# A four-layer encoder and a sparse-attention block on one core: later probability transposes, other banks for the attention results, a searched order of issue

## The chip, the cores and the metric

The kernel runs on one core of a Trainium2 chip as one launch. The metric is the device time of one execution in microseconds. Every time of the kernel before in this document comes from its measured runs or from the profile and the trace of one profiled execution.

## What is computed

The input is one sequence of 256 tokens of width 1024. Four layers follow each other; each is a mixer and a gated feed-forward net of hidden width 2816, with a layer norm behind either. The mixers are attention within a band of chunks (layers 0 and 3, 16 heads of 64), a gated linear attention with a running state (layer 1), and differential attention (layer 2, 8 pairs of maps, whose second map is taken off with a learned weight). Cut from the reference:

```
for i in range(DEPTH):
    if kind == 0:   y = chunk_band_attention(h, a_w_qkv[j], a_rel_bias[j], a_w_o[j])
    elif kind == 1: y = gated_linear_attention(h, ...)
    else:           y = differential_attention(h, ...)
    h = layer_norm(DN_ALPHA * h + y, ln1_g[i], ln1_b[i])
    h = layer_norm(DN_ALPHA * h + swiglu(h, ...), ln2_g[i], ln2_b[i])
```

A second block takes the result: a feed-forward net, then a mixer that picks for every query the 64 best keys by an index score and attends to these alone, beside a short convolution; then cross attention to 256 memory rows, and a last feed-forward net. All weights are float32 and are read once, in some 600 transfers of 512 KB.

## The kernel before

The 256 tokens are two tiles of 128, `tt` 0 and 1. `stream(tt)` (L1019) is a generator that writes down all the work of one tile, layer by layer, and gives control back after every quarter of a weight unit. `run` (L1053) lets tile 0 go ahead of tile 1: the lead grows from `LAG0` = 1 step by one step for every `LAGK` = 4 steps of tile 1, up to `LAG` = 6 (L32, L33).

A weight quarter is 512 KB. One SP transfer brings it into one of 5 `raw` buffers (L268); ACT copies it to `wh` in the fast fp32r format (L276), DVE takes the rest `wl` = raw - wh (L277), each in one of 10 buffers. The activations are split alike (`sth`, `stl`; `gth`, `gtl`). A product is then three matmuls of 128 x 512 (`mm3`, L288, L290, L292). `lin` (L294) makes 512 columns of a projection, `lin_out` (L310) the 1024 columns of an output projection. PSUM has eight banks: four with the tag `acc` for `lin_out`, two `lin` for `lin`, and two `at` for transposes and scores (L250). With a tag, banks are opened in the order in which the program was written down.

Attention for a group of heads goes like this in `mixer_attn` (L658). After the projection "q", the queries are transposed (`to_heads`). Then, twice (sub 0 and 1), `attn_probs` (L603) makes the scores of four heads in two `at` banks (L613, a burst that nothing may break up), adds the bias and takes the maximum on DVE (L619), takes the exponential on ACT (L624), and scales on DVE (L629, or L685 and L687 in layer 2); and at once `transpose_probs` (L632, matmul L641) turns the probabilities `p` over into `pt`. After the projection "v", the result `o` is made in a `lin` bank (L707, L715) and copied out of it (`bank_to_gt`, L350; in layer 2 to `t`, L720, with a norm behind it: squares L723, L530, a power on POOL L363, L534, L727). The gated layer keeps its result in a `lin` bank too (L804), and so does the cross attention (L1006). `mixer2` (L842) has the selecting attention: eight rounds of maximum and replace on DVE (L911, L912), then scores and probabilities as above, transposed at once and used after the projections "bo" and "sb0".

The order in which instructions are issued isn't the written one. `order_issue` (L1393) reads all instructions, and `plan_order` (L1162) makes a graph of them. `play` (L1227) plays the program once with fixed durations: the engine that can start first takes, of up to 24 candidates, the one with the earliest deadline. Deadlines are counted back from the times at which PE has to do its matmuls. `play` is run four times, the PE order of one round setting the deadlines of the next, and the best round's order is fixed for every engine. A transfer counts as its bytes by 360 per ns, whatever its rows (L1087). All transfers share SP's queue; loads that are not weights are the bias tiles (`b<-toep`, L483, 128 KB each, rows of 256), the bias tables in DRAM (`toep<-t`, L469), the norms' gains and offsets (`bc`, L369, 512 KB) and some small constants.

Of the kernel before, what the change touches and what calls it, by code (L numbers as in the profile page):

```python
# [32 lines left out]
LAG0, LAGK = 1, 4  # L33
# [176 lines left out]
class Net:  # L210
# [83 lines left out]
    def lin(self, st, key):  # L294
# [4 lines left out]
        for a in range(u.nq):  # L299
# [10 lines left out]
    def lin_out(self, gt, key, accs, first, last):  # L310
# [3 lines left out]
        for a in range(u.nq):  # L314
# [6 lines left out]
            if a == u.nq - 1:  # L321
                for b, wh, wl in kept:
                    self.mm3_out(gt, b, accs, (1,), wh, wl, first and b == 0, last and b == u.nq - 1)
            yield
# [333 lines left out]
    def mixer_attn(self, tt, st, i):  # L658
# [3 lines left out]
        for g in range(2):  # L662
# [8 lines left out]
            probs = []  # L671
            for sub in range(2):
# [7 lines left out]
                if diff:  # L680
# [17 lines left out]
            o = self.bank("lin")  # L698
# [36 lines left out]
    def mixer_gla(self, tt, st, i):  # L735
# [42 lines left out]
        for pr in range(2):  # L778
# [19 lines left out]
            o = self.bank("lin")  # L798
# [43 lines left out]
    def mixer2(self, tt, st):  # L842
# [87 lines left out]
        probs = []  # L930
# [52 lines left out]
    def cross(self, tt, st):  # L983
        nc = self.nc
        gts = []
        for g in range(2):
# [16 lines left out]
            o = self.bank("lin")  # L1003
# [84 lines left out]
DMA_BACKLOG = 2500.0  # L1088
TAIL = 10000.0
# [5 lines left out]
class Op:  # L1095
    __slots__ = ("inst", "eng", "dur", "fset", "preds", "succs", "opens", "idx", "dl", "npred", "ready", "start", "end",
                 "burst")
# [56 lines left out]
def _bytes(inst):  # L1154
    o = inst.outs[0]
    n = 4
    for s, c in list(o.ap):
        n *= c
    return n

# [66 lines left out]
def play(ops, users, tag_of, bufs_of, nominal):  # L1227
# [17 lines left out]
    loads = [op.idx for op in ops if op.eng == "SP" and op.inst.outs[0].bass_ap.tensor.name.startswith(("raw", "h0", "h1"))]  # L1245
    for i, j in zip(loads, loads[1:]):
        before[i].append(j)
    for op in reversed(ops):
# [4 lines left out]
        if op.eng == "SP":  # L1253
            d -= DMA_LAND + _bytes(op.inst) / DMA_RATE
# [8 lines left out]
        op.ready = 0.0  # L1263
    slots = {}
    for name, tag in tag_of.items():
        slots.setdefault(tag, [0.0] * bufs_of[tag])
    left = {name: len(u) for name, u in users.items()}
    done_at = {name: 0.0 for name in users}
    touched = [[] for _ in range(n)]
# [23 lines left out]
    def eff(op):  # L1293
# [9 lines left out]
        if op.opens:  # L1303
# [3 lines left out]
            for tag, k in need.items():  # L1307
# [3 lines left out]
                t = max(t, sorted(s)[k - 1])  # L1311
        return t
    while ndone < n:
# [47 lines left out]
        free[e] = t + dur  # L1361
        if e == "SP":
            dma_free = max(dma_free, t + DMA_ISSUE + 650) + _bytes(op.inst) / DMA_RATE
# [4 lines left out]
        order[e].append(i)  # L1368
# [99 lines left out]
```

## Time and profile before

| | us |
|---|---|
| median of 3 runs | 1912.93 |
| lowest to highest | 1912.18 to 1914.75 |
| the profiled execution, its own time | 1910.72 |
| its span, first to last instruction | 1908.9 |
| PE busy | 1873.2 |
| DVE busy | 1177.6 |
| ACT busy | 940.6 |
| mean granted share of PE's clock | 0.995 |

The page gives each engine's busy time. The timeline gives instructions in order of time; in brackets stands how long the engine sat idle before one, and what ended that. The view of stretches gives busy times and the granted clock of PE (1.00 is 2.4 GHz, 0.50 is 1.2 GHz) for pieces of the span. Matmuls are pipelined, so a matmul's own duration is longer than the time from one to the next.

### The profile page before, as it was taken

The page shows a single profiled execution, that of the slowest core. Times are in us where ns is not written, and L with a number is a line of the kernel's source. Part 1 is how long each engine was busy: PE and PEld are TensorE (multiplying, and loading weights), DVE is VectorE, ACT ScalarE, POOL GpSimd, SP SyncE. Part 2 cuts the span into 40 slices and gives each one's busy share as a digit, 9 for nine tenths or more (in the row PEclk, how much of TensorE's full clock was granted, in tenths as well). Part 3 has the DMA queues.
Part 4 walks back from the last instruction along what each step waited for, and adds up shares of the span by engine and source line. Part 5 has one row for each costly group of instructions (what it writes and reads, how often), then busy time and mean ns, then how long its engine had stood idle before and what let it go on. Part 6 is the DMA issues. An engine that isn't in the chain of part 4 may idle for free. (4 is left out here: it accounts for less than half of the span.)

```text
span 1908.9 us, 23804 instructions
## 1 busy us (share of the span) xinstructions
PE 1873.2 (98%) x8941; PEld 1519.8 (80%) x8941; DVE 1177.6 (62%) x1697; ACT 940.6 (49%) x1359; POOL 41.8 (2%) x65
## 2 busy tenths in 40 slices
PE   8899999999999999999999999999999899999998
PEld 7678887678888877888878888888877688788887
DVE  6576556567556777555767655765567867566554
ACT  6545445454444664444564444444445555545442
POOL 0000000000000000000000000000000000000000
PEclk9999999999999999999999999999999999999999
DMA  9546555656554645655554655465554466546662
GB/s 308 157 145 217 188 190 153 207 163 218 186 185 161 209 155 165 196 190 187 185 171 163 209 185 191 160 225 187 188 172 144 134 202 208 163 125 204 184 193 67
DMA packets 103437, 345.59 MB, mean 181 GB/s; under 512 B 13385, under 2 KB 20489, under 8 KB 103322
## 3 DMA queue, kind: packets, MB, share of 16 engines
q1 hardware_dynamic: 103322, 344.07, 56.4%
q8 instruction: 70, 1.15, 0.3%
q14 instruction: 45, 0.37, 0.1%
HBM read 341.01 MB, written 3.01 MB: 180 GB/s over the span
## 5 line engine op out<-in xcount | busy, mean ns | idle before, releaser
L277 DVE TENSOR_TENSOR wl<-raw,wh 128x1024 fp32r<-128x1024 f32 (+2 forms) x614 | 741.3, 1215 | 461.5 <-ACT wh L276 460.4
L276 ACT ACTIVATE wh<-raw 128x1024 fp32r<-128x1024 f32 (+2 forms) x614 | 643.6, 1053 | 640.2 <-PE lin L292 399.6
L288 PE MATMUL lin<-wh,sth 128*128 128x512 f32 x1696 | 665.0, 397 | 4.8 <-DVE t L856 1.3
L290 PE MATMUL lin<-wl,sth 128*128 128x512 f32 x1696 | 656.1, 392 | 1.1 <-DVE wl L277 1.1
L292 PE MATMUL lin<-wh,stl 128*128 128x512 f32 x1696 | 656.8, 393 | 0.0
L288 PEld LDWEIGHTS lin<-wh,sth 128*128 128x128 f32 x1696 | 318.4, 188 | 75.6 <-issue 5.2
L292 PEld LDWEIGHTS lin<-wh,stl 128*128 128x128 f32 x1696 | 318.4, 188 | 70.3 <-issue 5.3
L290 PEld LDWEIGHTS lin<-wl,sth 128*128 128x128 f32 x1696 | 318.8, 188 | 64.5 <-DVE wl L277 2.4
L290 PE MATMUL acc<-wl,gth 128*128 128x512 f32 x752 | 247.7, 394 | 0.0
L288 PE MATMUL acc<-wh,gth 128*128 128x512 f32 x752 | 244.7, 395 | 0.7 <-ACT gth L341 0.7
L292 PE MATMUL acc<-wh,gtl 128*128 128x512 f32 x752 | 245.0, 393 | 0.0
L290 PEld LDWEIGHTS acc<-wl,gth 128*128 128x128 f32 x752 | 141.2, 188 | 30.3 <-DVE wl L277 0.9
L292 PEld LDWEIGHTS acc<-wh,gtl 128*128 128x128 f32 x752 | 140.6, 188 | 30.0 <-issue 1.3
L288 PEld LDWEIGHTS acc<-wh,gth 128*128 128x128 f32 x752 | 140.0, 188 | 30.4 <-issue 1.5
L336 PE MATMUL at<-ident,t 128*128 128x128 f32 x564 | 92.9, 276 | 9.6 <-DVE t L727 2.9
L336 PEld LDWEIGHTS at<-ident,t 128*128 128x128 f32 x564 | 70.1, 142 | 31.7 <-issue 9.3
L593 DVE TENSOR_TENSOR t<-t,lin 128x512 f32<-128x512 f32 x60 | 41.2, 687 | 68.5 <-PE lin L292 68.5
L363 POOL TENSOR_TENSOR sm<-sm,small 128x1 f32<-128x1 f32 (+2 forms) x42 | 37.0, 880 | 1649.9 <-DVE sm L512 917.0
L341 ACT ACTIVATE gth<-at 128x512 fp32r<-128x512 f32 (+1 forms) x88 | 49.5, 563 | 46.8 <-PE at L336 46.7
L624 ACT ACTIVATE p<-p,sm 128x128 f32<-128x128 f32 (+1 forms) x112 | 49.6, 444 | 34.7 <-DVE sm L622 34.7
L342 DVE TENSOR_TENSOR gtl<-at,gth 128x512 fp32r<-128x512 f32 (+1 forms) x88 | 57.2, 650 | 9.9 <-ACT gth L341 6.8
L590 ACT ACTIVATE t<-lin 128x512 f32<-128x512 f32 x60 | 35.8, 596 | 48.7 <-PE lin L292 48.6
(165 smaller groups left out, 859.9 us busy)
## 6 DMA issues: line engine op xcount, KB each, us to landing
raw<-in_weights_dram SPq DMA_DIRECT2D x607, 512.0 KB, 3.6
b<-toep SPq DMA_DIRECT2D x40, 128.0 KB, 5.1
bc<-in_ln_g_dram SPq DMA_DIRECT2D x8, 512.0 KB, 3.8
bc<-in_ln_b_dram SPq DMA_DIRECT2D x8, 512.0 KB, 5.9
toep<-t SPq DMA_DIRECT2D x2, 768.0 KB, 11.6
h<-in_x_dram SPq DMA_DIRECT2D x4, 256.0 KB, 5.8
bc<-in_ffn_post_g_dram SPq DMA_DIRECT2D x2, 512.0 KB, 3.6
p<-in_mem_dram SPq DMA_DIRECT2D x2, 512.0 KB, 6.6
```

Of the source, the lines that this page charges most:

```text
L276: nc.scalar.activation(hi[:, c], src[:, c], AF.Copy)
L277: nc.vector.tensor_sub(lo[:, c], src[:, c], hi[:, c].bitcast(F32))
L288: nc.tensor.matmul(o, xh, w, start=first, stop=False)
L290: nc.tensor.matmul(o, xh, w, start=False, stop=False)
L292: nc.tensor.matmul(o, xl, w, start=False, stop=last)
L336: self.nc.tensor.transpose(b[:, k], src[:, k * 128:(k + 1) * 128], self.ident)
L341: self.nc.scalar.activation(hi, b[:, :n], AF.Copy)
L342: self.nc.vector.tensor_sub(lo, b[:, :n], hi.bitcast(F32))
L363: nc.gpsimd.tensor_tensor(out, x, self.mhalf[:, :x.shape[1]], op=OP.pow)
L590: nc.scalar.activation(gate[j], acc, AF.Silu)
L593: nc.vector.tensor_mul(s, s, acc)
L624: nc.scalar.activation(P[:, hh, :nk], P[:, hh, :nk], AF.Exp, bias=nm[:, hh:hh + 1], accum_out=sm[:, hh:hh + 1])
```

## The change

- The transposes of the probabilities are written later. `mixer_attn` makes both halves' probabilities first and hands a function `turn` to the projection "v", which calls it after its second quarter; in `mixer2` it is called after the last quarter of "bo".
- The results `o` of `mixer_attn`, of the gated layer and of `cross` are in an `at` bank instead of a `lin` bank. In `mixer2` it stays in `lin`.
- `LAGK` is 1, so tile 0's lead grows by a step for each step of tile 1.
- In `play`, a transfer with rows under 512 elements on either side counts at 110 per ns. A load that is neither a weight nor the input isn't issued before 30 us ahead of its deadline.
- `play` is run 60 times. After three rounds, `search` sorts what PE waited for by pieces of 40 us, and in later rounds takes off a random part of these waits from the deadlines of the instructions that caused them; by piece, the best set of such hurries is kept, and the order with the shortest end is used.

The matmuls themselves, the transfers and the work on DVE, ACT and POOL stay the same in number and size. The diff, without bookkeeping (who set an instruction's start, what buffer came free by whom):

```diff
-LAG0, LAGK = 1, 4
+LAG0, LAGK = 1, 1
...
-    def lin(self, st, key):
+    def lin(self, st, key, later=None, after=0):
...
+            if later is not None and a == after:
+                later()
             yield
...
-            probs = []
+            Ps, probs = [], []
...
-                    PT = self.transpose_probs(tt, P, (0, 2))
-                else:
-                    PT = self.transpose_probs(tt, P, range(4))
-                probs.append(PT)
-            acc = yield from self.lin(st, (i, "v", g))
+                Ps.append(P)
+
+            def turn():
+                for P in Ps:
+                    probs.append(self.transpose_probs(tt, P, (0, 2) if diff else range(4)))
+
+            acc = yield from self.lin(st, (i, "v", g), turn, 1)
             v = self.t("v2", [128, 512], 4)
             self.copy(v, acc)
             self.v[g, tt] = v
-            o = self.bank("lin")
+            o = self.bank("at")
...
-            o = self.bank("lin")
+            o = self.bank("at")
...
-            probs.append(self.transpose_probs(tt, P, range(4)))
+            Ps.append(P)
+
+        def turn():
+            for P in Ps:
+                probs.append(self.transpose_probs(tt, P, range(4)))
+
         for which in "ba":
             accs = [self.bank("acc"), self.bank("acc")]
-            yield from self.lin_out(gtb if which == "b" else gta, which + "o", accs, True, True)
+            yield from self.lin_out(gtb if which == "b" else gta, which + "o", accs, True, True,
+                                     turn if which == "b" else None, 3)
...
-            o = self.bank("lin")
+            o = self.bank("at")
...
+SHORT_ROW, SHORT_RATE = 512, 110.0
+HOLD = 30000.0
...
+def _transfer(inst):
+    short = min(list(o.ap)[-1][1] for o in (inst.outs[0], inst.ins[0])) < SHORT_ROW
+    return _bytes(inst) / (SHORT_RATE if short else DMA_RATE)
...
-            d -= DMA_LAND + _bytes(op.inst) / DMA_RATE
+            d -= DMA_LAND + _transfer(op.inst)
+        d -= urge.get(op.idx, 0.0)
...
+        if op.eng == "SP" and op.idx not in first_loads and not raws(op):
+            op.ready = max(0.0, op.dl - HOLD)
...
+def waits_by_region(ops, order):
+
+    behind, res = {}, {}
+    for seq in order.values():
+        for a, b in zip(seq, seq[1:]):
+            behind[b] = a
+    for a, b in zip(order["PE"], order["PE"][1:]):
+        gap = ops[b].start - ops[a].start - ops[a].dur
+        if gap < 20.0:
+            continue
+        r = res.setdefault(ops[b].region, [0.0, []])
+        r[0] += gap
+        i, n = ops[b].blame, 0
+        while gap > 100.0 and i is not None and ops[i].eng != "PE" and n < 40:
+            n += 1
+            if ops[i].blame is None:
+                r[1].append((i, gap))
+                i = behind.get(i)
+            else:
+                i = ops[i].blame
+    return res
+
+
+def search(ops, users, tag_of, bufs_of, nominal, rounds):
+
+    rng = random.Random(1)
+    urge, best = {}, None
+    kept = {}
+    for r in range(rounds):
+        got = play(ops, users, tag_of, bufs_of, nominal, urge)
+        if got is None:
+            break
+        if r < 3:
+            t2 = 0.0
+            for i in got[1]["PE"]:
+                t2 += ops[i].dur
+                nominal[i] = t2
+        if r == 2:
+            for op in ops:
+                op.region = int(op.dl // REGION)
+            for i in got[1]["PE"]:
+                ops[i].region = int(nominal[i] // REGION)
+        if best is None or got[0] < best[0]:
+            best = got
+        if r < 3:
+            continue
+        now = waits_by_region(ops, got[1])
+        tried = {}
+        for i, x in urge.items():
+            tried.setdefault(ops[i].region, {})[i] = x
+        for g in set(now) | set(kept):
+            w, causes = now.get(g, [0.0, []])
+            if g not in kept or w < kept[g][0] - 1.0:
+                kept[g] = (w, tried.get(g, {}), causes)
+        urge = {}
+        for g, (w, us, causes) in kept.items():
+            urge.update(us)
+            if r % 8 and r < rounds - 2:
+                size = rng.choice((0.3, 0.6, 1.0, 2.0))
+                for i, gap in causes:
+                    if rng.random() < 0.5:
+                        urge[i] = urge.get(i, 0.0) + min(gap, 2000.0) * size
+                for i in us:
+                    if rng.random() < 0.1:
+                        urge[i] *= 0.5
+    return best
...
-def order_issue(tc, nc, tag_of, bufs_of, bursts, rounds=4):
+def order_issue(tc, nc, tag_of, bufs_of, bursts, rounds=60):
...
-    best = None
-    for r in range(rounds):
-        got = play(ops, users, tag_of, bufs_of, nominal)
-        if got is None:
-            break
-        if best is None or got[0] < best[0]:
-            best = got
-        t2 = 0.0
-        for i in got[1]["PE"]:
-            t2 += ops[i].dur
-            nominal[i] = t2
+    best = search(ops, users, tag_of, bufs_of, nominal, rounds)
```

The order on PE, in the selecting attention of tile 0, from the second half's scores (L613, L618 in the change) to the transposes of its probabilities (L641, L646). Before:

```order
L613 MATMUL at_12307<-k_2572_11854,q_2673_12270 128x128
L613 MATMUL at_12308<-k_2572_11854,q_2673_12270 128x128
L290 MATMUL acc_12338<-wl_12360,gth_2631_12115 128x512
L292 MATMUL acc_12337<-wh_12359,gtl_2632_12116 128x512
L292 MATMUL acc_12338<-wh_12359,gtl_2632_12116 128x512
L288 MATMUL acc_12337<-wh_12390,gth_2631_12115 128x512
L288 MATMUL acc_12338<-wh_12390,gth_2631_12115 128x512
L641 MATMUL at_12331<-ident_63,p_2686_12313 128x128 x2
L336 MATMUL at_12371<-ident_63,t_2701_12369 128x128 x2
```

With the change, from the first half's scores on; the last row transposes the first half, and the second half follows 8 rows later:

```order
L618 MATMUL at_12277<-k_2572_11854,q_2673_12270 128x128
L618 MATMUL at_12278<-k_2572_11854,q_2673_12270 128x128
L289 MATMUL lin_12367<-wh_12140,sth_2539_11687 128x512
L291 MATMUL lin_12367<-wl_12141,sth_2539_11687 128x512
L293 MATMUL lin_12367<-wh_12140,stl_2540_11688 128x512
L289 MATMUL lin_12367<-wh_12229,sth_2539_11687 128x512
L291 MATMUL lin_12367<-wl_12230,sth_2539_11687 128x512
L618 MATMUL at_12300<-k_2572_11854,q_2673_12270 128x128
L618 MATMUL at_12301<-k_2572_11854,q_2673_12270 128x128
...
L291 MATMUL acc_12324<-wl_12377,gth_2631_12115 128x512
L293 MATMUL acc_12324<-wh_12376,gtl_2632_12116 128x512
L646 MATMUL at_12405<-ident_63,p_2677_12283 128x128 x4
```

The two halves' scores now stand five matmuls apart and ahead of everything that uses them; before, one half was transposed ahead of the next half's scores.

The order on SP in layer 1, the gated layer, where the bias tiles of layer 2 (`b_1115`, `b_1231`), a bias table and the norm's gains (`bc`) were loaded between weights. Before:

```order
L268 DMA raw_2879<-in_weights_dram 128x1024
L483 DMA b_1115_5200<-toep_2592 32x4x256 x3
L268 DMA raw_2897<-in_weights_dram 128x1024
L268 DMA raw_2927<-in_weights_dram 128x1024
L469 DMA toep_2597<-t_561_2594 512x1x384
L483 DMA b_1115_5200<-toep_2592 32x4x256
L268 DMA raw_2945<-in_weights_dram 128x1024
L483 DMA b_1231_5667<-toep_2592 32x4x256 x4
L369 DMA bc_3545<-in_ln_g_dram 128x1024
L369 DMA bc_3547<-in_ln_b_dram 128x1024
L268 DMA raw_2965<-in_weights_dram 128x1024
```

With the change, the same stretch of weights:

```order
L269 DMA raw_2840<-in_weights_dram 128x1024
L269 DMA raw_2879<-in_weights_dram 128x1024
L474 DMA toep_2597<-t_561_2594 512x1x384
L269 DMA raw_2897<-in_weights_dram 128x1024
L269 DMA raw_2927<-in_weights_dram 128x1024
L269 DMA raw_2945<-in_weights_dram 128x1024
L269 DMA raw_2965<-in_weights_dram 128x1024
L269 DMA raw_2983<-in_weights_dram 128x1024
L269 DMA raw_3031<-in_weights_dram 128x1024
```

Bias tiles and gains have left this stretch, and one bias table is left in it.

The order on DVE at the end of layer 2's attention, tile 1: the norm of the second group's result (L530, L534, L727; L535, L539, L734 in the change) and the layer norm of tile 0 (L508 to L512; L513 to L517). Before:

```order
L277 TENSOR_TENSOR wl_6176<-raw_6173,wh_6175 128x1024
L277 TENSOR_TENSOR wl_6194<-raw_6191,wh_6193 128x1024
L530 TENSOR_SCALAR sm_6054<-sm_6048 128x4
L534 TENSOR_SCALAR sm_6058<-sm_6055 128x4
L509 BN_STATS sm_6121<-h_15_77 128x6 x2
L510 BN_AGGR sm_6122<-sm_6121 128x2
L512 TENSOR_SCALAR sm_6129<-sm_6122 128x1
L727 SCALAR_TENSOR_TENSOR t_1325_6046<-t_1325_6046,sm_6058,cst_5000 128x128 x4
```

With the change:

```order
L278 TENSOR_TENSOR wl_6102<-raw_6099,wh_6101 128x1024
L278 TENSOR_TENSOR wl_6158<-raw_6155,wh_6157 128x1024
L535 TENSOR_SCALAR sm_6054<-sm_6048 128x4
L513 SCALAR_TENSOR_TENSOR h_15_77<-h_15_77,acc_5853 128x512
L539 TENSOR_SCALAR sm_6058<-sm_6055 128x4
L734 SCALAR_TENSOR_TENSOR t_1325_6046<-t_1325_6046,sm_6058,cst_5000 128x128 x4
L514 BN_STATS sm_6121<-h_15_77 128x6
L513 SCALAR_TENSOR_TENSOR h_15_77<-h_15_77,acc_5854 128x512
```

The statistics of the layer norm (BN_STATS, BN_AGGR) stood ahead of the scaling of `t`; now they stand behind it.

## Rows read from the trace of the kernel before

**Rows 1.** The page: the span, and PE's busy time with its share.

```profile
span 1908.9 us, 23804 instructions
...
PE 1873.2 (98%) x8941; PEld 1519.8 (80%) x8941; DVE 1177.6 (62%) x1697; ACT 940.6 (49%) x1359; POOL 41.8 (2%) x65
```

**Rows 2.** Stretches: us, each engine's busy us (instructions), PEclk, DMA share, GB/s.

```profile
60.00:70.00 10.00, 6.18 (x38) 5.06 (x38) 3.79 (x13) 3.87 (x11) 0.38 (x2) 0.72 0.60 158
70.00:80.00 10.00, 10.00 (x55) 8.19 (x52) 1.92 (x2) 2.37 (x4) 0.00 (x0) 0.94 0.18 54
340.00:350.00 10.00, 7.52 (x39) 5.75 (x37) 5.04 (x5) 6.97 (x10) 0.31 (x1) 1.00 1.03 361
...
550.00:600.00 50.00, 50.00 (x230) 41.32 (x229) 26.35 (x26) 22.80 (x25) 0.00 (x0) 1.00 0.56 183
...
730.00:740.00 10.00, 7.22 (x28) 5.32 (x29) 8.99 (x18) 3.22 (x5) 0.56 (x1) 0.83 0.11 34
1490.00:1500.00 10.00, 8.77 (x42) 5.94 (x40) 9.56 (x33) 3.19 (x10) 0.00 (x0) 1.00 0.53 156
1500.00:1510.00 10.00, 6.08 (x27) 4.13 (x29) 6.35 (x16) 5.97 (x14) 0.00 (x0) 0.66 0.13 31
```

**Rows 3.** Timeline, PE: start, us, form, count [idle before it <-releaser].

```profile
52.43 0.47 PE L288 MATMUL lin<-wh,sth 128*128 128x512 f32 x1 [1.32 <-DVE gtl L353]
...
56.36 1.23 PE L641 MATMUL at<-ident,p 128*128 128x128 f32 x8 [0.48 <-DVE p L629]
...
64.98 1.30 PE L641 MATMUL at<-ident,p 128*128 128x128 f32 x5 [3.82 <-DVE p L629]
...
349.51 0.65 PE L336 MATMUL at<-ident,t 128*128 128x128 f32 x4 [2.48 <-ACT sm L763]
...
680.08 0.50 PE L288 MATMUL lin<-wh,sth 128*128 128x512 f32 x1 [0.51 <-ACT t L720]
...
732.10 1.02 PE L336 MATMUL at<-ident,t 128*128 128x128 f32 x4 [2.85 <-DVE t L727]
733.81 1.22 PE L288 MATMUL acc<-wh,gth 128*128 128x512 f32 x2 [0.69 <-ACT gth L341]
...
1503.92 0.66 PE L641 MATMUL at<-ident,p 128*128 128x128 f32 x2 [5.15 <-DVE p L629]
```

**Rows 4.** Timeline, all engines: the first of the long stops, 58 to 65 us.

```profile
58.90 1.13 PE L613 MATMUL at<-k,q 64*128 64x256 f32 x8
...
60.07 0.42 DVE L619 CUSTOM_DVE_ANT_0 p<-at,b 128x256 f32<-128x256 f32 x1 [0.38 <-PE at L613]
...
61.83 0.51 ACT L624 ACTIVATE p<-p,sm 128x256 f32<-128x256 f32 x1
...
64.15 1.29 DVE L629 TENSOR_TENSOR p<-p,sm 128x512 f32<-128x512 f32 x2
```

**Rows 5.** Timeline, SP and ACT, 328 to 350 us, layer 1.

```profile
328.90 7.21 SPq L483 DMA_DIRECT2D b<-toep  x4
...
338.02 20.99 SPq L268 DMA_DIRECT2D raw<-in_weights_dram  x9
...
346.92 1.06 ACT L276 ACTIVATE wh<-raw 128x1024 fp32r<-128x1024 f32 x1 [2.85 <-DMA raw<-in_weights_dram]
347.99 1.28 ACT L763 ACT_TABLE_LOAD   x1
```

**Rows 6.** Timeline, ACT, POOL and DVE, 726 to 733 us, the end of layer 2's attention.

```profile
726.62 0.58 ACT L720 ACTIVATE t<-lin 128x512 f32<-128x512 f32 x1
...
728.86 1.01 POOL L363 TENSOR_TENSOR sm<-sm,small 128x4 f32<-128x4 f32 x1 [2.81 <-DVE sm L530]
...
729.98 1.28 DVE L509 BATCH_NORM_STATS2 sm<-h 128x6 f32<-128x512 f32 x2
...
731.61 1.13 DVE L727 SCALAR_TENSOR_TENSOR t<-t,sm,cst 128x128 f32<-128x128 f32 x4
```

**Rows 7.** The page's groups: the weight split on DVE.

```profile
L277 DVE TENSOR_TENSOR wl<-raw,wh 128x1024 fp32r<-128x1024 f32 (+2 forms) x614 | 741.3, 1215 | 461.5 <-ACT wh L276 460.4
```

More of the change, by code (lines that the diff above doesn't have):

```diff
@@ L2 @@
 import math
+import random
 from contextlib import ExitStack
@@ L306, in lin, with lin_out @@
                 self.mm3([acc[:, :n]], st[0][:, kt], st[1][:, kt], [wh[:, s]], [wl[:, s]], kt == 0, kt == 7)
+            if later is not None and a == after:
+                later()
             yield
         return acc
-    def lin_out(self, gt, key, accs, first, last):
+    def lin_out(self, gt, key, accs, first, last, later=None, after=0):
         u = self.by_key[key]
@@ L323, in lin_out @@
                     self.mm3_out(gt, b, accs, (1,), wh, wl, first and b == 0, last and b == u.nq - 1)
+            if later is not None and a == after:
+                later()
             yield
@@ L1096 @@
     __slots__ = ("inst", "eng", "dur", "fset", "preds", "succs", "opens", "idx", "dl", "npred", "ready", "start", "end",
-                 "burst")
+                 "burst", "blame", "region")
 def _region(o):
@@ L1224, in plan_order, with play @@
     return ops, users
-def play(ops, users, tag_of, bufs_of, nominal):
+def play(ops, users, tag_of, bufs_of, nominal, urge):
     inf = float("inf")
@@ L1245, in play @@
     loads = [op.idx for op in ops if op.eng == "SP" and op.inst.outs[0].bass_ap.tensor.name.startswith(("raw", "h0", "h1"))]
+    first_loads = set(loads)
+    raws = lambda op: op.inst.outs[0].bass_ap.tensor.name.startswith("raw")
     for i, j in zip(loads, loads[1:]):
@@ L1263, in play @@
         op.ready = 0.0
+        op.blame = None
+        if op.eng == "SP" and op.idx not in first_loads and not raws(op):
+            op.ready = max(0.0, op.dl - HOLD)
     slots = {}
     for name, tag in tag_of.items():
-        slots.setdefault(tag, [0.0] * bufs_of[tag])
+        slots.setdefault(tag, [(0.0, None)] * bufs_of[tag])
     left = {name: len(u) for name, u in users.items()}
     done_at = {name: 0.0 for name in users}
+    last_at = {}
     touched = [[] for _ in range(n)]
@@ L1310, in eff @@
                     return inf
-                t = max(t, sorted(s)[k - 1])
+                t = max(t, sorted(s, key=lambda x: x[0])[k - 1][0])
         return t
@@ L1361, in play @@
         free[e] = t + dur
+        delays = [(op.ready, op.blame)]
         if e == "SP":
-            dma_free = max(dma_free, t + DMA_ISSUE + 650) + _bytes(op.inst) / DMA_RATE
+            dma_free = max(dma_free, t + DMA_ISSUE + 650) + _transfer(op.inst)
             op.end = dma_free + DMA_LAND
@@ L1368, in play @@
         order[e].append(i)
+        freed = []
         for name in op.opens:
             tag = tag_of[name]
-            slots[tag].sort()
-            slots[tag].pop(0)
+            slots[tag].sort(key=lambda x: x[0])
+            freed.append(slots[tag].pop(0))
             turn[tag] += 1
             opens.setdefault(tag, []).append(i)
+        x, who = max(delays + freed, key=lambda y: y[0])
+        op.blame = who if x > t - 1.0 else None
         for name in touched[i]:
             left[name] -= 1
-            done_at[name] = max(done_at[name], op.end)
+            if op.end >= done_at[name]:
+                done_at[name], last_at[name] = op.end, i
             if left[name] == 0:
-                slots[tag_of[name]].append(done_at[name] + 220.0)
+                slots[tag_of[name]].append((done_at[name] + 220.0, last_at[name]))
         for j in op.succs:
             s = ops[j]
-            if s.preds[i]:
-                s.ready = max(s.ready, op.end + (SELF[e] if s.eng == e else LAT[e]))
-            else:
-                s.ready = max(s.ready, t)
+            x = op.end + (SELF[e] if s.eng == e else LAT[e]) if s.preds[i] else t
+            if x >= s.ready:
+                s.ready, s.blame = x, i
             s.npred -= 1
```

3 lines of the change are left out of this document (2 added, 1 removed).

## Prediction

> **What bounds the kernel now.** I read the page first. PE is busy for 1873.2 of 1908.9 us [rows 1], so PE is the bound from end to end, and a change that keeps its matmuls can win only in two places: where PE stands still, and where it runs at half its clock. Idle time is 1908.9 - 1873.2 = 35.7 us. The view of stretches gives the second: PEclk is 0.72 and 0.94 in two stretches of 10 us behind 60 us, 0.83 at 730 and 0.66 at 1500 [rows 2]. The share that is missing, times 10 us, is 2.8 + 0.6 + 1.7 + 3.4 = 8.5 us of full-speed work, lost inside "busy" time. So 44 us, 2.3%, is all that order could ever give. Third comes the timeline of PE, for the stops one by one [rows 3]. They are few. Three wait for probabilities at their transpose (L641): 0.48, 3.82 and 5.15 us. Two wait to open a `lin` bank that holds an attention result until it is copied out (L353, L720): 1.32 and 0.51 us. One of 2.48 us waits in the gated layer for a decay on ACT, and the end of layer 2's attention costs 2.85 + 0.69 us. These eight are 17.3 us. The remaining 18.4 us are the start, the end and small stops; I count on nothing there. The three falls of the clock lie at the three longest stops (60 to 70, 730 to 740, 1500 to 1510), and at no other; beside the stop of 2.48 us the clock stays at 1.00 [rows 2, 3].
>
> **The change, term by term.** PE has the same 8604 matmuls before and after, and the groups of slow float32 ones among the fast ones are as many (315 and 313, counted in the two orders), so PE's work is the same. What moves is the distance between work and what it needs.
>
> *Probabilities.* The chain from scores to transpose is in the timeline: scores end at 58.90 + 1.13 = 60.03, the reductions on DVE start at 60.07, the first exponential at 61.83, the scaling at 64.15, the transpose at 64.98 [rows 3, 4]. That is 4.95 us. In full stretches PE does 230 instructions in 50 us, so about 0.22 us each [rows 2]. In the order before, 4 matmuls stand between scores and transpose at this place and 5 at the one of 1503.92, so 0.9 and 1.1 us of cover for some 5 us; at the other 26 places it is 17 or more. With the change the same two have 31 and 34, and the smallest of all 28 is 17 (3.7 us, for 128 keys, where four reductions and exponentials are shorter; places with 17 didn't stop PE before). 31 x 0.22 = 6.8 us covers 4.95 with 1.9 to spare. I take all three stops off: 9.45 us. Bounds: 0 if the scores come as much later as the transposes, 9.45 at most.
>
> *Banks.* The results no longer stand in `lin`, so the next projection needn't wait for the copy: 1.32 + 0.51 = 1.83 us off. What is late next is an `at` bank, which is held by the result in its place; in the new order at least 1.6 us of other work stands ahead of whoever opens it next. The nearest row for such a wait is the same 1.32 [rows 3], so the bounds are 0 and 1.83; I take the gain whole, since 1.6 covers 1.32.
>
> *SP's queue in layer 1.* Four bias loads keep SP from 328.90 to 336.11, the gains follow, and weights are issued only from 338.02. ACT then sits 2.85 us until a weight lands at 346.92, with the table load and the decay queued behind it, and PE stops 2.48 us for that decay [rows 3, 5]. With the change the bias tiles go to where their layers begin, one by one between weights, and the gains behind this stretch; one table write is left. ACT's wait then has no cause. Off: 2.48 us (bounds 0 and 2.48).
>
> *The norm in layer 2.* From the copy at 726.62 to the transposes at 732.10 the chain has 5.5 us, of which DVE spends 729.98 to 731.61 on the layer norm's statistics, ahead of the scaling that PE waits for [rows 3, 6]. In the new order the statistics stand behind it. That gives back up to 1.63 us, and the transposes of this norm, which had as little as 2.7 us of other work ahead of them, now have 4.3 at all four places (matmuls counted in the order, at 0.22). 1.63 + 1.6 = 3.2 against stops of 2.85 + 0.69; I take off 3.5, bounds 1.6 and 3.54.
>
> *The clock.* If no stop of 2.8 us or more is left, the clock has no cause to fall, and 8.5 us come back. Bounds 0 and 8.5; I take 8.5, since each fall lies at a stop taken off above.
>
> Together 9.45 + 1.83 + 2.48 + 3.5 + 8.5 = 25.8 us.
>
> *What it adds: score pairs.* In 14 places the second half's scores now follow the first half's after 7 matmuls (5 or 6 with 128 keys, where the reductions are shorter), and they open the same two `at` banks, which are free only when DVE has reduced the first half. The room is 7 x 0.22 = 1.54 us; the reductions take at most 61.83 - 60.07 = 1.76 us [rows 4]. So each pair waits between 0 and, if a weight split of 1.22 us stands ahead on DVE [rows 7], 1.76 + 1.22 - 1.54 = 1.44 us. Behind the waiting scores stands every matmul. I take 0.3 us, near the case without a split: 14 x 0.3 = 4.2 us lost (bounds 0 and 20).
>
> *DVE in the selecting attention.* From 1490 to 1510 DVE is busy 9.56 + 6.35 = 15.9 of 20 us [rows 2]. I took 5.15 + 3.4 = 8.55 us off there, which leaves 11.45 us for that work; unless splits move out of the stretch, it gives only 20 - 15.9 = 4.1. The loss lies between 0 and 4.45 us. The splits can move, since ten buffers stand ahead, and the waiting DVE work is ordered anew; I take 2 us.
>
> *The head.* With `LAGK` 1 tile 0 needs weights sooner, but the gains, the constants and a table of rows of one element leave the first 60 us of the queue. By bytes ahead in the queue over the work ahead on PE, the new order asks for no more than the old one did in its first 16 us (0.33 MB per us), and for 0.28 at most later. The five `raw` and ten split buffers hide what is left, so I count nothing; without that cover a late weight costs what ACT waited for one in layer 1, 2.85 us [rows 5].
>
> Sum: 25.8 - 4.2 - 2 = 19.6 us. The profiled execution took 1910.72 us by itself (1.8 around its span); the median is 1912.93. So the same execution would take 1891.1, and the median **1893 us**, 1.0% less.
>
> **The rivals.** A measurement of this kernel can tell about 0.2% from no change, 3.8 us.
>
> *Half of it.* In the selecting attention DVE is the bound: top-k, splits and softmax are one chain, PE stops there as before and the clock falls. For it: 9.56 of 10 us busy [rows 2]. Against it: DVE idles behind the stretch. Then the 8.55 us stay, less the 2 that I charged: 1893.3 + 6.6 = **1900 us**.
>
> *It doesn't do what it says.* The search counts stops on the plan's own clock and may fit that alone. On the chip, stops come from what the plan doesn't know (a weight that lands late [rows 5]), and move elsewhere. For it: the order before was the best of its plan too, and left 17.3 us. Against it: the two orders differ at just these stops. Then **1912 us**, within 0.2%.
>
> *Slower: score pairs and the clock.* A split stands ahead of the reductions in each pair, PE stops 1.44 us 14 times, 20.2 us, and where stops come in such pairs the clock falls, each time for the 3.4 us that the fall at 730 lasts (0.17 x 10 us lost), 1.7 us. Without any fall the kernel still gains 25.8 - 2 - 20.2 = 3.6 us; with n falls it takes 1912.9 - 3.6 + 1.7 x n, so it is slower from three falls on and by over 0.2% from five; with eight, **1923 us**. Against it: the stretch with a single stop of 2.48 us keeps its clock at 1.00, and a pair is shorter [rows 2]. The Trainium skill (TensorE: Matmul & The Clock Gate, section "A second HAM failure mode: psum-queue depth-cycling") says that a kernel which cycles through PSUM banks leaves PE idle for moments often enough that its clock swings between its two levels, and such bank cycling is what the pairs do. By that rule all 14 pairs would cost a fall, and the time would be 1933 us; the trace doesn't bear it out so far, since of the eight stops listed only the three longest have a fall beside them.
>
> **How the numbers follow.** My forecast 0.72, its own range 1885 (no loss by pairs or DVE, and 2 us of the small stops) to 1898 (pairs at 0.65 us); half of it 0.17; nothing 0.06; slower 0.05. To hold 8 in 10 the range takes in the second case with some more loss by pairs: **1885 to 1904**. Faster by over 0.2% is 0.72 + 0.17 = 0.89, within it 0.06, slower 0.05.
>
> **What would show it.** In the profile of the changed kernel: PE's idle time falls from 35.7 to some 24 us; the timeline of PE has no stop at the probability transposes of over 0.5 us, none at a `lin` bank held by a result, and none of 2 us in layers 1 and 2; PEclk is 1.00 in all stretches but the last. Each fall that is left costs 1.7 to 3.4 us. The pairs are wrong if the second half's scores show idle time ahead that is released by the reductions, of more than 0.3 us in the mean. DVE in the selecting attention is wrong if that stage still holds a stop of over 2 us. The forecast as a whole is wrong if new stops, at other lines than these, add up to over 8 us.

## The result, and the profile after

The changed kernel takes **1880.26 us** in the median of four runs (1878.24 to 1880.63), beside 1912.56 for the kernel before in the same session. The ratio is 0.9829, with a 95% interval of 0.9812 to 0.9846: 32 us less, where 20 were forecast. The time lies below the range. The profiled execution took 1880.37 us, which is like its median; that of before took 1910.72.

The page after, span and PE, to set beside [rows 1]:

```profile
span 1878.6 us, 23806 instructions
...
PE 1864.3 (99%) x8941; PEld 1515.6 (81%) x8941; DVE 1174.8 (63%) x1697; ACT 939.6 (50%) x1359; POOL 44.4 (2%) x65
```

Idle time of PE is 1878.6 - 1864.3 = 14.3 us; it was 35.7. So of 30.3 us less span, 21.4 are stops that went and 8.9 are busy time. That nearly all of the busy time is the clock's shows in the stretches (columns as in [rows 2]): three of before's stretches, the end of layer 2's attention, which now lies at 720 to 730, and the selecting attention, now at 1460 to 1490:

```profile
60.00:70.00 10.00, 10.00 (x61) 8.26 (x61) 8.54 (x21) 6.84 (x16) 0.61 (x2) 1.00 0.94 245
70.00:80.00 10.00, 10.00 (x77) 7.86 (x74) 8.02 (x28) 4.90 (x13) 0.00 (x0) 1.00 0.86 277
340.00:350.00 10.00, 10.00 (x48) 7.84 (x47) 5.50 (x7) 3.42 (x4) 0.00 (x0) 1.00 0.62 195
720.00:730.00 10.00, 10.00 (x46) 8.25 (x46) 9.17 (x14) 3.89 (x5) 0.00 (x0) 1.00 0.88 308
1460.00:1470.00 10.00, 8.80 (x49) 6.39 (x49) 9.49 (x36) 4.23 (x8) 0.00 (x0) 1.00 0.09 19
1470.00:1480.00 10.00, 9.74 (x48) 7.08 (x45) 9.96 (x30) 6.92 (x19) 0.00 (x0) 1.00 0.57 189
1480.00:1490.00 10.00, 9.71 (x55) 6.50 (x54) 9.02 (x22) 5.48 (x10) 0.00 (x0) 1.00 0.59 163
```

PEclk is 1.00 in all of them, and in the first four PE is full. What PE still waits for is in the view of waits (who waits, for whom: us in all, times, longest):

```profile
PE at L341 <- DVE t L577: 2.1, 7, 0.4
PE acc L401 <- DVE t L398: 1.5, 1, 1.5
PE lin L289 <- ACT wh L277: 1.2, 1, 1.2
PE lin L289 <- DVE t L846: 1.2, 1, 1.2
PE at L341 <- ACT t L660: 0.7, 1, 0.7
PE at L341 <- DMA h<-in_x_dram: 0.5, 1, 0.5
PE at L341 <- ACT t L653: 0.3, 1, 0.3
PE at L618 <- ACT q L653: 0.3, 1, 0.3
PE acc L291 <- DVE wl L278: 0.2, 1, 0.2
```

In all it is 8.0 us, of which 3.8 (L398, L277, `h`, L660) are the first 20 us of the kernel; 6.3 us behind the last matmul make up the rest. No probability transpose (L646) is in the list, no bank that holds a result, nothing of layers 1 and 2. All eight stops of [rows 3] are gone.

### The profile page after: what moved, and what is told of

Read it like the earlier page. It is cut to its first block, busy times and chain, and to the rows that moved or that the text cites. A ratio compares the mean times of both kernels' runs of the same rounds, so it can differ in the third digit from the quotient of the medians.

```text
span 1878.6 us, 23806 instructions
## 1 busy us (share of the span) xinstructions
PE 1864.3 (99%) x8941; PEld 1515.6 (81%) x8941; DVE 1174.8 (63%) x1697; ACT 939.6 (50%) x1359; POOL 44.4 (2%) x65
## 4 chain that ended last, share of the span: by engine, by line
PE 95%; DVE 3%; ACT 1%; issue 1%; DMA 1%; POOL 1%; SPq 0%; DVEq 0%; POOLq 0%; ACTq 0%
PE lin L289 20%; PE lin L291 20%; PE lin L293 20%; PE acc L291 9%; PE acc L293 9%; PE acc L289 8%; PE at L341 4%; PE at L618 1%; PE at L646 1%; PE at L714 1%; POOL sm L368 1%; DVE wl L278 0%; ACT t L549 0%; PE at L1007 0%; PE at L1019 0%
## 5 line engine op out<-in xcount | busy, mean ns | idle before, releaser
L277 ACT ACTIVATE wh<-raw 128x1024 fp32r<-128x1024 f32 (+2 forms) x614 | 644.0, 1053 | 646.0 <-PE lin L293 415.5
L289 PE MATMUL lin<-wh,sth 128*128 128x512 f32 x1696 | 665.9, 396 | 2.4 <-ACT wh L277 1.2
L289 PEld LDWEIGHTS lin<-wh,sth 128*128 128x128 f32 x1696 | 318.8, 188 | 69.4 <-issue 4.7
L289 PE MATMUL acc<-wh,gth 128*128 128x512 f32 x752 | 243.1, 394 | 0.0
L289 PEld LDWEIGHTS acc<-wh,gth 128*128 128x128 f32 x752 | 139.7, 188 | 29.1 <-issue 0.6
L341 PE MATMUL at<-ident,t 128*128 128x128 f32 x564 | 90.8, 273 | 3.1 <-DVE t L577 2.1
L341 PEld LDWEIGHTS at<-ident,t 128*128 128x128 f32 x564 | 69.2, 140 | 24.6 <-issue 3.8
```

The costliest lines, as they stand in the source:

```text
L277: nc.scalar.activation(hi[:, c], src[:, c], AF.Copy)
L289: nc.tensor.matmul(o, xh, w, start=first, stop=False)
L341: self.nc.tensor.transpose(b[:, k], src[:, k * 128:(k + 1) * 128], self.ident)
```

## The experiments

Ratios are to the kernel before in the same session, with 95% intervals; the changed kernel has 0.9829. A point is 0.01 of such a ratio, some 19 us. The structure is the lead, the late transposes and the banks; a fall is a stretch in which the granted clock drops to half.

| run | what it has | ratio (95%) |
|---|---|---|
| e2 | before + search | 0.9994 (0.9982 to 1.0005) |
| e8 | before + lead 1 for 1 | 0.9990 (0.9981 to 1.0000) |
| e7 | before + load rules | 0.9976 (0.9967 to 0.9986) |
| e14 | before + search + load rules | 0.9955 (0.9941 to 0.9968) |
| e11 | late transposes, lead | 0.9939 (0.9923 to 0.9955) |
| e4 | late transposes, lead, banks | 0.9905 (0.9879 to 0.9931) |
| e3 | changed, without load rules | 0.9866 (0.9852 to 0.9881) |
| e1 | changed, without search | 0.9861 (0.9843 to 0.9878) |
| e5 | changed, transposes early | 0.9894 (0.9879 to 0.9909) |
| e6 | changed, results in `lin` | 0.9909 (0.9893 to 0.9924) |
| e13 | as e6, other seed | 0.9886 (0.9872 to 0.9900) |
| e10 | changed, other seed | 0.9845 (0.9829 to 0.9861) |
| e15 | changed, 200 rounds | 0.9837 (0.9824 to 0.9851) |
| e16 | changed, plan with net switch price | 0.9846 (0.9833 to 0.9860) |
| e12 | changed, plan with full switch price | 0.9869 (0.9853 to 0.9885) |
| e9 | changed, pairs made tight | 0.9891 (0.9876 to 0.9906) |

**The parts.** "No search" is four plays; "no load rules" and the lead are numbers:

```diff
-def order_issue(tc, nc, tag_of, bufs_of, bursts, rounds=60):
+def order_issue(tc, nc, tag_of, bufs_of, bursts, rounds=4):
...
-SHORT_ROW, SHORT_RATE = 512, 110.0
-HOLD = 30000.0
+SHORT_ROW, SHORT_RATE = 0, 110.0
+HOLD = 1e12
```

e1: 

> The changed kernel with the plan played 4 times and no hurrying, all else as changed. Theory A (the late transposes and the banks take off the stops at probabilities and banks with their clock falls, the load rules the stop of layer 1; the search only collects small stops): 1882 to 1888 us, no stop of over 0.5 us at the probability transposes, PEclk 1.00 inside. Theory B (the search does most of it, the rest only gives it room): 1895 us or more, with stops of over 1 us back at probabilities or in layer 2's norm and at least one fall of the clock.

e3: 

> The changed kernel without the two load rules: a transfer counts at 360 per ns whatever its rows, and no load is held back. Theory A: bias loads gather in SP's queue again, so a weight lands late and PE stops some 2.5 us in layer 1: 1883 us (1881 to 1886). Theory B (the search hurries what is late, whatever the load rules): 1880 us within 2. A third possibility, that the held-back loads alone keep the first 60 us free: stops of together over 5 us return before 70 us and the clock falls there, 1888 us or more.

e4 (both of these together): 

> Late transposes, the at banks for results and the lead growing by 1 for 1, with no search and without the load rules. Theory A: the stops at probabilities (9.45 us), at banks (1.83) and two falls of the clock (6.8) go, those of layer 1 and layer 2's norm stay: 1912.9 - 18 = 1895 us (1891 to 1899). Theory B: stops only move, 1903 us or more. If the score pairs cost anything that the search hid, the timeline shows idle time ahead of the second half's scores here, up to 1.4 us a pair.

e1 took 1884.91 us, e3 1886.02, e4 1893.54. The structure alone is worth 0.95 points, 18 us. On top of it the load rules give 0.44 points (e4 to e1), the search 0.39 (e4 to e3), and little less when the other is there (0.37, 0.32): 7 to 8 us and 6 to 7. Four rows and the changed kernel, read in this order, add one part each: the lead (e8) 0.10 points, the late transposes (e11) 0.51, the banks (e4) 0.34, the load rules (e1) 0.44, the search (the changed kernel) 0.32. Each step is known to some 0.2 to 0.3 points, so the lead's is within the noise, the transposes' is well clear of it, and the others only just.

e1's time lies in theory A's range, but A's signs did not come: at 1478.95 a probability transpose waits 1.61 us, then `acc` 0.72, and the clock is 0.83 there. e3 has the stop of layer 1 back (2.37 us, clock 0.83), as A said, and came out above A's range by 0.02 us. e4's time is A's, but layer 2's norm, which A left as it was, has no stop in it. e8 still stops 2.85 us there, at 732.27, and e11 does not; these two differ by the transposes alone.

In e4 the only score pair that waits is the first, and not for the length of its reductions but for their bias tile. The timeline of e4, SP, DVE and PE:

```profile
28.71 5.03 SPq L488 DMA_DIRECT2D b<-toep  x8
...
35.93 0.29 DVE L624 CUSTOM_DVE_ANT_0 p<-at,b 128x128 f32<-128x128 f32 x1 [2.31 <-DMA b<-toep]
...
36.71 1.22 PE L618 MATMUL at<-k,q 64*128 64x128 f32 x8 [2.91 <-DVE sm L624]
```

Eight bias loads in a row, and the first reduction gets its tile at 35.93. The load rules take away that stop and the one of layer 1 (2.10 us in e4), each with a fall of the clock: 2.91 + 2.10 + 2 x 1.7 = 8.4 us, beside 8.6 between the medians of e4 and e1. (The two profiled executions differ by 10.8; 2.1 us of that are stops in the selecting attention.) I had counted 2.5.

**Parts without the rest.** e2, e14, e7 and e8 leave the transposes, banks and, but for e8, the lead as before.

e2: 

> The kernel before with the search alone: transposes early, results in the lin banks, lead growing by 1 for 4, load rules of before, plan played 60 times. Theory A: 1897 to 1908 us, since the two places with 4 and 5 matmuls between scores and transposes stay as they are written; stops of 3 us or more at the probability transposes and falls of the clock remain. Theory B: 1880 to 1888 us, and those stops are gone.

e14: 

> The kernel before with the search and the load rules, without the structure (transposes early, results in lin, lead 1 for 4). In this order the smallest numbers of matmuls between scores and transposes are 6, 10 and 15; with the search alone 4 and 5. Theory A (the search gains nothing as long as the order of the at banks is written with the transposes at once): 1902 to 1909 us, the load rules' 5 us and little more, with stops of over 2 us at the transposes. Rival (the load rules are what the search lacked): 1895 us or less.

e7: 

> The kernel before with the two load rules alone (no search, transposes early, results in lin, lead 1 for 4). Theory A: the stop of 2.5 us in layer 1 goes, the stops at probabilities stay: 1905 to 1911 us. Rival (late loads at the head are what made the stops at the first probabilities too): 1902 us or less, with less than 2 us of stops between 50 and 70 us.

e8: 

> The kernel before with the lead of tile 0 growing by 1 for 1, alone. Theory A: the lead only changes which work stands between, and by itself takes off no listed stop for certain: 1907 to 1916 us. Rival (the longer lead is what separates the two tiles' attention, so that the 4 and 5 matmuls become 17 or more): 1900 us or less, and no stop over 1 us at the probability transposes in layer 0.

The search alone gives nothing (1909.78 us, 1.8 above A's range). The waits of e2:

```profile
PE at L646 <- DVE p L634: 9.1, 3, 4.6
PE at L341 <- ACT sm L766: 2.2, 1, 2.2
PE at L618 <- ACT q L653: 2.1, 1, 2.1
PE lin L289 <- DVE gtl L358: 2.0, 1, 2.0
```

All known stops are there; in its order, 4 and 5 matmuls stand between scores and transposes at the two places, as before. Banks of a tag are opened as written, and the search can't put other scores between. With the load rules (e14, 1901.67 us) 3.6 us at L646 are left, in stops of 1.89 and 1.68; the time is just under A's range and far from the rival's. So beside the load rules the search does give something without the structure: 0.21 points from e7 to e14, some 4 us, only just clear of the noise. Of the structure alone without the lead nothing was tried. e7 and e8 came out within A (1907.87 and 1910.39).

**Taking one part out.**

```diff
-            acc = yield from self.lin(st, (i, "v", g), turn, 1)
+            acc = yield from self.lin(st, (i, "v", g))
```

e5, with `probs.append(self.transpose_probs(...))` in the loops again: 

> The changed kernel with the transposes of the probabilities written early again, all else as changed. Theory A (they are what takes off the stops at probabilities): stops of 3 us or more come back at two probability transposes, with falls of the clock: 1892 to 1898 us. Rival (with the held-back loads and the search the early transposes find cover too): within 3 us of the changed kernel.

e5 took 1891.3 us, 11 more than the changed kernel and just under A's range, but not by the stops that A named: one of 5.04 us stands at 723.43, in layer 2's norm (L341 from `t` L730), with a fall that costs 3.4 us. The two probability stops are 1.07 and 0.49 us. So with the search and the load rules the early transposes do find most of their cover, as the rival said, but not its time: most of the loss stands at the norm, whose stop the late transposes take off in e11 too.

```diff
-            o = self.bank("at")
+            o = self.bank("lin")
```

e6, in all three places: 

> The changed kernel with the attention results in the lin banks again. Theory A: the waits for a copied bank return, 1.3 to 2.5 us in all: 1882 to 1885 us, with stops at L289 ended by the copies. Rival (the later transposes and the longer lead leave enough other work, so the bank does nothing): 1880 us within 2.

e13, the same with `random.Random(2)`: 

> The changed kernel with the results in the lin banks and seed 2 of the search. Theory A (the banks' direct price is 1.5 to 2.5 us; the rest of the 13 us was one order's luck in the selecting attention): 1882 to 1887 us, under 4 us of stops between 1450 and 1500 us. Rival (results in lin take away the freedom that the search needs there): 1890 us or more, again with 5 us or more of stops and a fall of the clock in that stage.

e11, the same with neither search nor load rules: 

> As the run with the structure alone (1893.5 us), but with the results in the lin banks: late transposes and the longer lead only. Theory A (the banks' direct price is the wait for the copy, 1.3 to 2.5 us, and the 13 us of the searched order with lin banks were the search's luck in the selecting attention): 1895 to 1897 us. Rival (the lin banks by themselves cost 10 us or more, by holding up the projections behind them): 1903 us or more.

e10, the changed kernel with the other seed: 

> The changed kernel with another seed of the search (2 instead of 1). Theory A (the search finds what there is): 1880 us within 3, the selecting attention with stops of under 2.5 us and no fall of the clock there. Rival (what the search gained in the selecting attention is luck of one order, as the 6.9 us of stops there with results in lin suggest): 1885 to 1893 us, with stops of over 3 us and a fall of the clock between 1450 and 1500 us, none of it elsewhere.

Results in `lin` cost 14 us in e6 (1894.28), where A said 2 to 5; 7.7 in e13 (1887.98), or 6.5 beside e10, which has its seed; 4.9 in e11 against e4 (1898.44), or 6.5 by the ratios. The small waits for a bank that holds a result are some 1.4 us in each. In e6 the rest stands in the selecting attention, whose result is in `lin` in every kernel: 5.2 us more of stops than in the changed kernel, and two falls. In e13 the stops there are 2.0 us more, without a fall; in e11 they are no more than in e4. The waits of e6, then of e13:

```profile
PE lin L291 <- DVE wl L278: 2.6, 2, 2.1
PE lin L289 <- DVE t L846: 2.6, 1, 2.6
```

```profile
PE lin L289 <- DVE t L846: 2.9, 2, 2.7
```

The changed kernel has 1.2 us at this line. With results in `at` the second seed does well (e10, 1881.5 us), so two seeds agree there; with results in `lin` neither does well, though one by 6 us less than the other. e13 misses both ranges, A's by 1 us; A's signs for the stage, under 4 us of stops and no fall, did come. So the price is more than the direct wait, and part of e6's 14 us was its order. Why a bank that is used elsewhere makes this stage later was not settled.

**The score pairs.** The forecast charged 4.2 us for them. The timeline of a pair after (PE, then DVE):

```profile
691.05 1.14 PE L618 MATMUL at<-k,q 64*128 64x256 f32 x8
692.12 0.50 PE L291 MATMUL lin<-wl,sth 128*128 128x512 f32 x1
...
693.37 0.61 PE L289 MATMUL acc<-wh,gth 128*128 128x512 f32 x2
693.92 1.13 PE L618 MATMUL at<-k,q 64*128 64x256 f32 x8
```

```profile
692.22 0.42 DVE L624 CUSTOM_DVE_ANT_0 p<-at,b 128x256 f32<-128x256 f32 x1 [0.45 <-PE at L618]
...
693.26 0.42 DVE L624 CUSTOM_DVE_ANT_0 p<-at,b 128x256 f32<-128x256 f32 x1
...
693.80 1.22 DVE L278 TENSOR_TENSOR wl<-raw,wh 128x1024 fp32r<-128x1024 f32 x1
```

The scores end at 692.19; the reductions run from 692.22 to 693.68; the next scores start at 693.92. So the seven matmuls last 1.73 us (0.25 each), the reductions 1.46, and 0.24 us are to spare; the split stands behind. Of thirteen such pairs (the forecast counted 14) nine show seven matmuls and the others 5, 8 or 9, and none waits for its reductions. To see what a pair costs without that room, e9 tells the plan a shorter time:

```diff
+        if type(inst).__name__ == "InstCustomDveAnt" and inst.outs[0].bass_ap.tensor.name.startswith("p4"):
+            op.dur *= 0.3
```

> The changed kernel, with the plan told that the four reductions of the scores take 0.3 of their time, so that 3 or 4 matmuls instead of 7 stand between the scores of the first and second half at 9 places (6 or 8 at four others). Theory A (the pairs cost nothing only because the plan puts in as many matmuls as the reductions last; each one less costs about its 0.25 us, beyond the 0.25 us to spare): stops of about 0.5 us at 8 or 9 second halves, 4 to 5 us in all, no fall of the clock: 1884 to 1886 us. Rival of the prediction (stops at pairs let the clock fall): falls in layers 0, 2 and 3 as well, 1895 us or more. Null (something else covers the pairs): 1880 us within 2.

e9 took 1889.66 us. The same kind of pair in its timeline:

```profile
694.39 1.14 PE L618 MATMUL at<-k,q 64*128 64x256 f32 x8
...
696.25 0.39 PE L291 MATMUL lin<-wl,sth 128*128 128x512 f32 x1
696.73 1.47 PE L618 MATMUL at<-k,q 64*128 64x256 f32 x8
```

The second scores start 0.48 us behind the start of the last matmul ahead of them instead of 0.32, and take 1.47 us instead of 1.13, since they start while the last reduction still runs (DVE):

```profile
696.60 0.42 DVE L624 CUSTOM_DVE_ANT_0 p<-at,b 128x256 f32<-128x256 f32 x1
```

So such a pair loses 0.5 us: six do, and two more lose 0.3 to 0.4, some 4 us as expected. Hardly any of it is booked as idle time (0.09 us here): PE's busy time rises to 1869.7 us, 5.4 more than after, at the same clock; the pairs explain some 3 of these, and where the others come from was not looked at. 3.0 us of idle time come on top, two thirds of it at the transposes behind, whose probabilities are late. Together it is 8.4 us between the profiled executions, so e9 came out 3.7 us above theory A's range, by what A did not name, and below its rival's. No clock fell at the pairs; two of the stretches:

```profile
690.00:700.00 10.00, 9.91 (x52) 7.30 (x51) 7.63 (x22) 6.32 (x15) 0.46 (x1) 1.00 0.47 152
950.00:960.00 10.00, 9.49 (x50) 6.63 (x49) 6.74 (x24) 4.50 (x15) 0.30 (x1) 1.00 0.49 158
```

**A better order?** e15 is `rounds=200`. e12 and e16 add to `play` a price for PE's change between float32 and fp32r, and go on with the kind that runs:

```diff
+KEEP, SWITCH = 1500.0, {True: 95.0, False: 40.0}
...
+            same = [(y, j) for y, j in now if fast[j] == last_fast]
+            if same:
+                y, j = min(same)
+                if last_fast is False or y - dl < KEEP:
+                    dl, i = y, j
```

e12: 

> The changed kernel with a plan that counts the change between float32 and fp32r matmuls: 95 ns for the first fp32r matmul behind a float32 one, 40 ns the other way, and that stays with the kind that runs while what it passes over has a deadline less than 1.5 us earlier. In the trace of the changed kernel the first fp32r matmul behind a change takes 326 ns to the next, the later ones 227 to 234. 486 changes of kind stand in this order, 626 in the changed one: 70 groups fewer of 0.1 to 0.19 us give 7 to 13 us if nothing else gets later: 1867 to 1873 us. Rival (work held back by 1.5 us makes new stops at transposes): 1880 us or more, with stops of over 1 us at L341 or L646.

e16, with 0 and {16, 36} as numbers: 

> The changed kernel with a plan that counts a change of matmul kind at its net price (16 ns into fp32r, 36 ns into float32: the long first interval behind a change is mostly made up for by the short last one before it) and goes on with a kind while one is ready, without holding anything back. 566 changes instead of 626 at some 26 ns each are 1.6 us: 1878 to 1880 us. Rival (the price is the 135 ns of the earlier count): 1873 to 1876 us.

e15: 

> The changed kernel with 200 rounds of the search instead of 60. If the stops that are left (8.0 us, of which 3.8 at the start) can be found by the plan: 1877 to 1879 us. If they come from what the plan doesn't know, or are at the start and the end: 1880 us within 2.

None beats the changed kernel: 1886.0, 1881.65 and 1879.26 us for e12, e16 and e15 (e15 within the changed kernel's interval, and in the second of its two ranges). In e12 my price was wrong: in the mean, the last float32 matmul ahead of a fast one takes 33 ns to the next start instead of 112, so most of the 95 ns is only booked on the other side; with some 36 ns that the last fast matmul ahead of a group takes longer, the net is 36 + 95 - 79 = 52 ns a group. Even that wasn't got: PE is busy for 1865.2 us, 0.9 more than after, and a new stop of 1.84 us stands at 319.54, at a line that the expected text did not name. e16 missed both of its ranges and is no better than no change.

## Why the prediction was too high

The profiled execution was forecast at 1891.1 us and took 1880.37: 10.7 us short. Idle time was to fall by 17.3 - 4.2 - 2 = 11.1 us and fell by 21.4; busy time by 8.5 and fell by 8.9. The other 2 us, between the medians, are the step from this execution to the median, which the changed kernel doesn't have. The signs named for the stops and the clock came; idle time, 14.3 us where some 24 were named, did not.

- **Probabilities, 9.45 us: right.** Seen in the waits after: nothing at L646. From e8 to e11, which differ by the late transposes alone, the ratio falls by 0.51 points, some 10 us. In e11 and e4 3.1 and 4.4 us at L646 are left, in the selecting attention; there the search was needed too (see DVE below). e5 loses 11 us without the late transposes, though at another place.
- **Banks, 1.83 us: right as a stop, too small as a price.** The direct waits are of that size; taken out of the finished kernel, the banks cost 8 to 14 us (e13, e6), and in e11 5.
- **SP's queue, 2.48 us: right for layer 1, too narrow.** The load rules also keep the first reductions from waiting for their bias tiles (e4), a stop that the order before does not have.
- **Layer 2's norm, 3.5 us, and the clock, 8.5 us: right in size.** What takes off the norm's stop is that the probabilities' transposes are written later (e8, e11); the forecast went by the new order and did not ask which part made it, and the order of the statistics was not tried alone. The reason given for the clock, that only stops of 2.8 us or more make it fall, was not (below).
- **Score pairs, "I take 0.3 us", 4.2 us: mis-sized, it is 0.** Two of its numbers were off. A matmul in such a row takes 0.25 us, not 0.22, and the reductions last 1.46 us, not the 1.76 up to the exponential [rows 4]; room of 1.73 against 1.46 is cover, where I read 1.54 against 1.76. The plan knows the reductions' length, and puts seven there because seven do; told a shorter length, it puts four (e9), and the pairs then cost what that room avoids.
- **DVE in the selecting attention, "I take 2 us": mis-sized, it is 0.** I bounded DVE's share from 20 us [rows 2]. Over 60 us there was room, as the stretches show, of before (from 1450) and then of after (from 1440):

```profile
1450.00:1510.00 60.00, 52.92 (x276) 39.96 (x276) 50.99 (x139) 32.30 (x57) 0.30 (x1) 0.94 0.34 102
```

```profile
1440.00:1500.00 60.00, 57.96 (x291) 43.50 (x290) 55.85 (x156) 36.65 (x69) 1.16 (x1) 1.00 0.45 143
```

  DVE is busy for 55.85 us instead of 50.99, and PE gets 5 us more done. The longest stop left there is 1.2 us at L289, for DVE (L846). Without the search this term would have been paid: e4 stops 1.35 + 3.06 us there, e1 1.61 + 0.72, each with a fall.
- **"The remaining 18.4 us ... I count on nothing there": wrong by 4.1 us.** The end is the same 6.3 us in both; the other 12.1 became 8.0. In the selecting attention 2.5 of them became 2.0, elsewhere 9.6 became 6.0. Most of that is the structure's: e4, without the stops of it named above, has 6.6 elsewhere. Beside the load rules the search takes a part: e1 has 8.0 elsewhere, with 0.85 us at 658, 1.42 at 1412 and 0.46 at 1220, where the changed kernel has 0.40 at 1410 and nothing at the others. Two of the parts that went are in the view of waits before:

```profile
PE at L613 <- ACT q L648: 2.0, 1, 2.0
...
PE lin L288 <- ACT v L807: 0.6, 2, 0.3
```

  The first, at 30.84, is gone with the lead alone (e8). The second is of the small waits for a `lin` bank, 1.4 us with those of 0.52 and 0.28 about the cross attention; they stand in e11 and not in e4.

4.2 + 2 + 4.1 = 10.3 us is the whole shortfall of idle time. The three rivals fell: half of it by the profile after, with 2.0 us of stops, none over 1.2, and no fall left in that stage; that the search fits only its own plan by e1 against the changed kernel, though for the search alone it holds (e2); the slower case by e9. The Trainium skill (TensorE: Matmul & The Clock Gate, section "A second HAM failure mode: psum-queue depth-cycling") tells of a kernel whose clock swings because it cycles through PSUM banks with short pauses between its groups of matmuls. No run here shows that: in the changed kernel the pairs have no pause, in e9 eight of them have one, and PEclk is 1.00 in both. Eight pauses in 1887 us are few, so this does not speak against the page.

## What to carry to other kernels

When a change puts work closer together, measure the room and the work in it over the same interval and at the spacing that this mix of instructions has, and ask whether the planner that places them knows these lengths: if it does, it will fit them. A planner's search is worth what the written order lets it move; on the kernel before sixty rounds gave nothing, beside the load rules some 4 us, and behind the moved transposes and banks some 6. And a wait need not show as idle time: a burst that takes 1.47 us in place of 1.13 is one.

## What was not expected of the chip

**A stop's length alone does not tell whether the clock falls.** In the 18 profiles each of the 14 stops of 2.85 us or more behind the first 20 us has a fall beside it. Below that both occur: e13 stops 2.74 us at 1468.83 and keeps 1.00; e14 stops 1.59 us at 43.93 and falls to 0.83. The stretches of e13, then of e14:

```profile
1460.00:1470.00 10.00, 7.13 (x30) 5.26 (x29) 9.75 (x28) 3.67 (x4) 0.00 (x0) 1.00 0.34 105
```

```profile
40.00:50.00 10.00, 8.04 (x36) 5.82 (x36) 7.75 (x18) 5.87 (x14) 0.00 (x0) 0.83 0.47 144
```

So the 8.5 us came back because the stops went, and a stop of 1.6 us would already have put 1.7 of them at risk.

**The change between float32 and fp32r matmuls costs little.** In the changed kernel the mean first fast interval behind a change is 326 ns instead of 227 to 234, but the last slow one ahead of it 33 instead of 112.
